# Near scores of a banded attention as products of 32 query columns, with merge loads, merges and strided items at other steps

## The chip, the cores and the metric

The kernel runs on one core of a Trainium2 chip. The metric is the device time in microseconds (us) of one execution, the median of three runs. Engines are named as in the profile: PE is TensorE's matmul, PEld its weight load, DVE is VectorE, ACT is ScalarE, POOL is GpSimd, SP is SyncE, whose queue issues nearly all DMAs here. A row's "L890" is line 890 of the kernel before; the changed kernel's lines are one less from L898 to about L1182.

## The reference, cut to what matters

The reference is one decoder layer for a prompt of 2048 positions and for a small group of samples: norm, one input projection, eight attention heads of width 64 beside a gating unit, an output projection, a SwiGLU feed-forward part. The change lies in the prompt's attention. Each head has three branches with keys at distances 0, d, 2d, ..., w:

```
BRANCHES = ((128, 1), (512, 4), (2048, 16))
...
    s = jnp.einsum('bnqrhc,bnkrhc->bnrhqk', qb, kc).astype(jnp.float32)
    s = s * (HEAD_DIM ** -0.5) + bias_hj[None, None, None]
    s = jnp.where(valid[None, :, None, None], s, NEG_INF)
    lse = jax.nn.logsumexp(s, axis=-1)
    p = jnp.exp(s - lse[..., None])
    o = jnp.einsum('bnrhqk,bnkrhc->bnqrhc', p.astype(vc.dtype), vc)
...
    w = jax.nn.softmax(jnp.stack(lses, axis=0), axis=0)
    return jnp.sum(w[..., None] * jnp.stack(outs, axis=0).astype(jnp.float32), axis=0)
```

The last two lines merge the branches by weights that come from their softmax denominators.

## The kernel before, in words

The program has three parts: the input projection with the samples' attention (to about 561 us of the span), the prompt's attention (561 to 862 us), and the output projection with the feed-forward part (to the end).

**The attention part** works on head pairs p = 0 to 3, two heads of 64 channels side by side in the 128 partitions. A pair has 16 band items n = 0 to 15 of 128 query positions each, which do the branches with d = 1 and d = 4 together, and four strided items "s" of 512 positions, which do the branch with d = 16. Query columns are kept by residue modulo 4: in an item's 128 columns, r * 32 to r * 32 + 31 are the positions of residue r.

A band item passes these steps, all of whose names stand in its rows of the profile:
- `pair_scores`: the scores in one tile `ps_s` for both heads z. "Near" keys are the 256 of this and the preceding block (128 where n is 0), for all 128 query columns of a head in one product (L890). "Far" keys are up to 96 of the same residue in the three blocks before; each residue has its own, so a product takes 32 query columns (L897) and there are four per head. Items n = 0 and 1 have no far keys.
- `band_bias` on DVE (L903) adds the bias and takes the minimum, `band_exp` on ACT, `band_turn` on PE (transposes, L919) with copies on ACT and DVE.
- `band_values` on PE: products with `ve`, the values by block (L942), and with `vf`, the values of far keys (L952); `band_out` copies to `ob`.

A strided item reorders k and q on POOL (`strided_order`, tile `sq`, L967), multiplies (L977), adds the bias and takes minima on DVE, subtracts these on POOL (`strided_sub`, L989, tile `e`), takes exp on ACT (L992), transposes on PE (L1001), multiplies with the values, and copies to `o`.

After a pair's last item the merge weights are worked out from its statistics (`Stats`, tile `f`), stored to the DRAM tile `f_d` (L1073) and read back spread over partitions (`merge_load`, L1087, four calls of two DMAs). A merge is three POOL operations on 256 columns of the pair: L1096 multiplies `ob` by its weight, L1098 multiplies `o`, L1100 adds. After four merges `merge_store` writes half of `ob` to `cat_d` (L1104), which the output projection reads.

**The order** is written out by a plan: `at(step, phase, fn)` puts a call at a step, and within a step phases go in a fixed order. Each engine, and SP's queue of DMA issues, runs its instructions in the order in which the plan issues them. A pair takes NI = 40 steps, two for each item, starting at B0 for p = 0; the items' order is one of the lists `FIRST` (p = 0), `OTHER` (p = 1, 2) and `LAST` (p = 3). The merges of pair p run during the items of pair p + 1, counted in steps from that pair's start, s0. The next pair's tiles are loaded during a pair by five calls of `load`: q, k, the bias b, v by residue, and `ve` in four DMAs. `sgu_sample_cat_load` is a DMA of the samples' gating result (`pair<-cs_d`, L1112), whose transposes on PE stand at step B0 + 22 (L1119). `pair` is a tag with two buffers, used by that load and by the merge loads.

Of the kernel before, what the change touches and what calls it, by code (L numbers as in the profile page):

```python
# [10 lines left out]
F32 = mybir.dt.float32  # L11
# [8 lines left out]
P = 128  # L20
T = 2048
NT = T // P
# [3 lines left out]
C = 64  # L26
# [10 lines left out]
FAR = 96  # L37
BAND = FAR + 2 * P
# [7 lines left out]
class Plan:  # L46
# [8 lines left out]
    def at(self, step, phase, fn, *args):  # L55
        self.events.append((step, self.PHASES.index(phase), self.n, fn, args))
        self.n += 1
# [10 lines left out]
def hymba_step(ctx: ExitStack, tc: tile.TileContext, A: dict, O: dict):  # L68
    nc = tc.nc
    sync, act, dve, pool, pe = nc.sync, nc.scalar, nc.vector, nc.gpsimd, nc.tensor  # L70
# [11 lines left out]
    def ps_s():  # L82
        return psum_s.tile([P, 2, 512], F32, name="ps_s", tag="s", bufs=2)
# [84 lines left out]
    at = plan.at  # L168
# [7 lines left out]
    def pair_tile(dtype=F32R):  # L176
        return rp.tile([P, 2, 512], dtype, name="pair", tag="pair", bufs=2)
# [481 lines left out]
    B0 = 240  # L659
# [4 lines left out]
    for n in range(len(first) + 4):  # L664
        if n >= 4:
            (w_split if first[n - 4][0] == "w" else x_half_split)(*first[n - 4][1:])
        if n < len(first):
            if first[n][0] == "w":
                k = first[n][1]
# [41 lines left out]
    for half in range(2):  # L711
        for ki, kind in enumerate(ORDER[half]):
            for gi, tiles in enumerate(GROUPS):
                start = ((half * 5 + ki) * 3 + gi) * 8
# [72 lines left out]
    i = 0  # L787
# [91 lines left out]

    def pair_scores(*its):  # L880

        d, s = its[0]["d"], ps_s()
        for z, it in enumerate(its):
            n = it["n"]
            m = min(3, max(0, n - 1))
            near = P if n == 0 else 2 * P
            it.update(s=s[:, z, :], c0=FAR - 32 * m if n else FAR + P, m=m)
            half = slice(z * C, z * C + C)
            k0 = (n + 1) * P - near
            pe.matmul(it["s"][:, BAND - near:BAND], d["q"][half, n * P:(n + 1) * P], d["k"][half, k0:k0 + near], start=True, stop=True)  # L890
        for r in range(4):
            for z, it in enumerate(its):
                n, m, half = it["n"], it["m"], slice(z * C, z * C + C)
                if m:
                    k = d["k"][half].rearrange("p (n r i) -> p n r i", r=4, i=32)[:, n - 1 - m:n - 1, r, :]
                    c = n * P + r * 32
                    pe.matmul(it["s"][r * 32:r * 32 + 32, it["c0"]:FAR].rearrange("p (n i) -> p n i", i=32),  # L897
                              d["q"][half, c:c + 32], k, start=True, stop=True)  # L898

    def band_bias(it):  # L900
        d, st, n, z, s, c0 = (it[x] for x in ("d", "st", "n", "z", "s", "c0"))
# [177 lines left out]
    def merge_load(p, j):  # L1079

        if p < HP - 1:
            f = pair_tile(F32)
            t_ = f[:, 0], f[:, 1]
        else:
            t_ = raw_tile(), zn_tile()
        for c in range(2):
            sync.dma_start(t_[c], dap(f_d, (p * 8 + j + c) * 2 * CP * 512, [[512, 2 * CP], [0, C // CP], [1, 512]]))  # L1087
            v = t_[c].rearrange("p (i z r) -> p i z r", z=2, r=NT)
            mf[p, j + c] = v[:, :, 0], v[:, :, 1]
# [45 lines left out]
        (strided_scores if its[0]["kind"] == "s" else pair_scores)(*its)  # L1135

    FIRST = [0, 1, 2, 3, "s", 4, 5, "s", 6, 7, 8, "s", 9, 10, 11, "s", 12, 13, 14, 15]
    OTHER = [0, "s", 1, 2, 3, 4, "s", 5, 6, 7, 8, "s", 9, 10, 11, 12, "s", 13, 14, 15]
    LAST = ["s", 0, 1, "s", 2, 3, "s", 4, 5, "s", 6, 7] + list(range(8, NT))
    units, taken = [], set()  # L1140
    for p in range(HP):
        r4 = 0
# [20 lines left out]
    for p in range(1, HP):  # L1163
        s0 = B0 + (p - 1) * NI
        at(s0 + 4, "misc", begin, p)
        for y in (4, 6, 8, 15, 18):
            at(s0 + y, "misc", load, p)

    def stats_of(p, steps, r0, r1):
# [5 lines left out]
    for p in range(HP):  # L1175
        s0 = B0 + (p + 1) * NI
        if p == HP - 1:
            x = s0 - NI
            stats_of(p, [(x + y, ph) for y, ph in ((26, "early"), (27, "turn"), (28, "early"), (28, "early"), (29, "early"), (29, "mid"))], 0, 64)
            steps = ((2, "early"), (2, "turn"), (3, "early"), (4, "early"), (5, "early"), (5, "early"))  # L1180
            for j in (0, 2):
                at(x + 30, "mid", merge_load, p, j)  # L1182
            for j, y, eng in ((0, 33, dve), (1, 33, pool), (2, 36, dve), (3, 36, pool)):
                for part in range(3):
                    at(x + y + part, "store", merge, p, j, eng, part)
            at(x + 36, "store", merge_store, p, 0, 2)
            at(x + 39, "store", merge_store, p, 2, 4)
        else:
            steps = ((2, "misc"), (3, "misc"), (4, "early"), (5, "early"), (5, "misc"), (6, "mid"))
            fast = p == HP - 2  # L1190
            y0 = 12
            when = [y0 + (i * 2 // 3 if fast else i) for i in range(24)]
            for j in range(0, 8, 2):
                at(s0 + max(8, when[3 * j] - 4) + (j == 2), "mid", merge_load, p, j)
            for i, y in enumerate(when):
                at(s0 + y, "store", merge, p, i // 3, pool, i % 3)
            for j in (0, 4):
                at(s0 + when[3 * j + 11] + 1, "store", merge_store, p, j, j + 4)
        stats_of(p, [(s0 + y, ph) for y, ph in steps], 64 if p == HP - 1 else 0, P)
# [34 lines left out]
    for n in range(3):  # L1234
        at(B0 + 40 + 30 * n, "store", down_plain, n)

    at(B0 + 19, "misc", sgu_sample_cat_load)
    at(B0 + 22, "scores", sgu_sample_cat)

    plan.run(B0)  # L1240
# [1270 lines left out]
```

## The time and the profile before

| what | value |
|---|---|
| runs | 2467.05, 2467.8, 2472.98 us; median 2467.8 us |
| profiled execution | 2461.96 us, its span 2460.2 us |
| granted TensorE clock over the span | 0.974 |
| attention part, by head pair (p = 0, 1, 2, 3) | 68.8, 74.1, 73.5, 84.1 us |
| PE busy over the span | 2350.1 us in 14592 records |
| POOL, DVE, ACT busy over the span | 1438.1, 1482.7, 1203.3 us |

The pairs' stretches are cut where PE reaches a pair's first scores, at 561.5, 630.3, 704.4 and 777.9 us; the last one ends at 862 us, where the output projection is running. In rows of groups, "out<-in" gives the tiles by the program's names, "x" the count, and the bracket the idle time ahead of an instruction with what ended it. "PEclk" is the granted clock as a share of full speed. A time "A:B" is in us from the span's start.

### The profile page before, as it was taken

To read this page: it belongs to the slowest core of one execution; us is meant where nothing else is said; L and a number is where in the kernel's file an instruction comes from. 1 tells how busy PE (TensorE), PEld (TensorE's weight loads), DVE (VectorE), ACT (ScalarE), POOL (GpSimd) and SP (SyncE) were. 2 spreads that over 40 slices of the span, in tenths; PEclk is the share of its full clock that TensorE was granted. 3 is DMA by queue.
4 is the path that set the end of the run, shared out by engine and by line. 5 is a ranking of instruction groups with operands and counts; after the bars stand their busy time and mean duration, and the time that the engine had idled before them with its cause. 6 is when DMAs were issued, how large, how long until landed. Compare 5 with 4: busy or idle time off the path is not lost. (4 is left out here: it accounts for less than half of the span.)

```text
span 2460.2 us, 41718 instructions
## 1 busy us (share of the span) xinstructions
PE 2350.1 (96%) x14592; PEld 2026.5 (82%) x14592; DVE 1482.7 (60%) x2902; ACT 1203.3 (49%) x2745; POOL 1438.1 (58%) x1153
## 2 busy tenths in 40 slices
PE   8999999997988899999999999999999998999998
PEld 6877786665666678999999988999999977999997
DVE  3467573114555534767777676566666666677676
ACT  6424333224555546656665546444443446555555
POOL 2225463112345646888788764756666563888885
PEclk9999999998989898999999999999999998999999
DMA  9864856786554564887877654766666644878552
GB/s 276 248 193 138 247 160 212 226 255 172 143 149 119 153 199 137 256 265 229 256 243 232 209 164 152 262 205 215 200 214 216 212 125 164 271 244 249 172 171 88
DMA packets 333365, 494.61 MB, mean 201 GB/s; under 512 B 42903, under 2 KB 174176, under 8 KB 329572
## 3 DMA queue, kind: packets, MB, share of 16 engines
q1 hardware_dynamic: 326308, 479.90, 63.4%
q10 hardware_dynamic: 6848, 12.06, 1.8%
q8 instruction: 115, 1.88, 0.3%
q14 instruction: 94, 0.77, 0.1%
HBM read 404.72 MB, written 168.98 MB: 233 GB/s over the span
## 5 line engine op out<-in xcount | busy, mean ns | idle before, releaser
L1626 POOL TENSOR_TENSOR op<-fr,op 128x512 fp32r<-128x512 f32 x392 | 522.5, 1342 | 350.6 <-ACT op L1622 262.1
L1863 PE MATMUL ps_m<-xh,op 128*128 128x384 f32 (+3 forms) x1344 | 429.9, 320 | 3.9 <-DVE raw L1874 3.5
L1864 PE MATMUL ps_m<-xl,op 128*128 128x384 f32 (+3 forms) x1344 | 428.6, 319 | 1.6 <-POOL xl L145 1.5
L1865 PE MATMUL ps_m<-xh,op 128*128 128x384 f32 (+3 forms) x1344 | 429.0, 319 | 0.0
L1716 DVE TENSOR_TENSOR acc<-acc,ps_o 128x512 f32<-128x512 f32 x448 | 300.3, 684 | 71.1 <-PE ps_o L1714 63.8
L1714 PE MATMUL ps_o<-hop 128*128 128x512 f32 x1142 | 322.6, 394 | 1.7 <-DVE hop L1695 1.0
L1863 PEld LDWEIGHTS ps_m<-xh,op 128*128 128x128 f32 x1344 | 256.7, 191 | 13.2 <-DVE raw L1874 6.7
L1864 PEld LDWEIGHTS ps_m<-xl,op 128*128 128x128 f32 x1344 | 256.4, 191 | 7.3 <-POOL xl L145 2.0
L1865 PEld LDWEIGHTS ps_m<-xh,op 128*128 128x128 f32 x1344 | 256.3, 191 | 0.0
L1714 PEld LDWEIGHTS ps_o<-hop 128*128 128x128 f32 x1142 | 209.4, 188 | 37.7 <-DVE hop L1695 2.8
L1622 ACT ACTIVATE op<-fr 128x512 fp32r<-128x512 f32 x396 | 239.3, 621 | 0.0
L325 PE MATMUL ps_s<-wh,xh 128*128 128x512 f32 x480 | 197.1, 411 | 6.1 <-ACT xh L142 6.0
L326 PE MATMUL ps_s<-wl,xh 128*128 128x512 f32 x480 | 190.0, 396 | 0.0
L327 PE MATMUL ps_s<-wh,xl 128*128 128x512 f32 x480 | 189.7, 395 | 0.0
L1863 PE MATMUL ps_t<-xh,op 128*128 128x384 f32 (+2 forms) x560 | 180.7, 323 | 5.5 <-ACT xh L1512 2.5
L1864 PE MATMUL ps_t<-xl,op 128*128 128x384 f32 (+2 forms) x560 | 179.9, 321 | 0.5 <-DVE xl L1534 0.3
L1865 PE MATMUL ps_t<-xh,op 128*128 128x384 f32 (+2 forms) x560 | 179.9, 321 | 0.0
L546 POOL TENSOR_TENSOR pr<-kv,qb 96x512 f32<-96x512 f32 x32 | 46.5, 1452 | 158.1 <-DMA kv<-in_cache_k_dram 77.0
L1695 POOL TENSOR_TENSOR hop<-hop 128x512 fp32r<-128x512 f32 x96 | 130.9, 1364 | 11.9 <-ACT hop L1691 11.4
L325 PEld LDWEIGHTS ps_s<-wh,xh 128*128 128x128 f32 x480 | 91.6, 191 | 41.4 <-issue 16.8
L1714 PE MATMUL ps_m<-hop 128*128 128x512 f32 x384 | 119.5, 392 | 0.0
L1877 ACT ACTIVATE zn<-zn 128x384 f32<-128x384 f32 (+2 forms) x65 | 31.6, 487 | 171.5 <-DVE zn L1876 171.5
(568 smaller groups left out, 5391.3 us busy)
## 6 DMA issues: line engine op xcount, KB each, us to landing
fr<-ab_d SPq DMA_DIRECT2D x308, 256.0 KB
hop<-dd_d SPq DMA_DIRECT2D x143, 256.0 KB
out_ks_dram<-in_cache_k_dram SPq DMA_DIRECT2D x56, 512.0 KB
out_vs_dram<-in_cache_v_dram SPq DMA_DIRECT2D x56, 512.0 KB
ab_d<-fr SPq DMA_DIRECT2D x88, 256.0 KB
dwx<-dd_d SPq DMA_DIRECT2D x71, 256.0 KB
ab_d<-pair SPq DMA_DIRECT2D x63, 256.0 KB
kv<-in_cache_k_dram SPq DMA_DIRECT2D x64, 192.0 KB
```

The costliest lines, as they stand in the source:

```text
L325: pe.matmul(o[j], xh[:, k, :], wh, start=(k == 0), stop=False)
L326: pe.matmul(o[j], xh[:, k, :], wl, start=False, stop=False)
L327: pe.matmul(o[j], xl[:, k, :], wh, start=False, stop=(k == KD - 1))
L546: eng.tensor_mul(pr[0:n], x[0:n], q[0:n])
L1622: act.activation(ops[f, j][0], ab[f][j], AF.Copy)
L1626: (pool if f > 1 or j in POOL_LOW[f] or B.b0 else dve).tensor_sub(lo_, ab[f][j], hi.bitcast(F32))
L1695: (pool if B.b0 or k >= 7 * (NF // 2 - 1) else dve).tensor_sub(lo_, lo_.bitcast(F32), hi.bitcast(F32))
L1714: pe.matmul(ps, l_, r_, start=(new and y == 0), stop=(y == 2), skip_group_check=True)
L1716: dve.tensor_add(x[:, cs], x[:, cs], ps)
L1863: pe.matmul(out, wh[:, ks], xh[:, :, k], start=(k == 0 and q not in (2, 4, 6)), stop=False, skip_group_check=True)
L1864: pe.matmul(out, wh[:, ks], xl[:, :, k], start=False, stop=False, skip_group_check=True)
L1865: pe.matmul(out, wl[:, ks], xh[:, :, k], start=False, stop=(k == 3), skip_group_check=True)
```

## The change

It has two parts. The near scores of an item are issued as four products of 32 query columns per head, each with all 256 (or 128) near keys, in the way of the far ones; first the eight near products, then the eight far ones. And calls stand at other steps:
- strided items come later in a pair's list (`OTHER`: after items 2, 6, 9 and 12 in place of 0, 4, 7 and 11; `LAST`: not at its head);
- `sgu_sample_cat_load` stands at B0 + 2 in place of B0 + 19;
- the four `merge_load` calls of a pair stand at s0 + 7 to s0 + 10 in place of four steps ahead of their merges, the later two in a new tile `mf` with two buffers; the merges start at s0 + 15 (14 for p = 2) in place of s0 + 12;
- the next pair's first three loads (q, k, b) stand at s0 + 11, 12, 13 in place of 4, 6, 8, where p > 1;
- in the last pair's merges, two that were DVE's are POOL's, at other steps, and the store of two is split in two.

The diff:

```
     def pair_scores(*its):
-        d, s = its[0]["d"], ps_s()
+        d, s, n = its[0]["d"], ps_s(), its[0]["n"]
+        m = min(3, max(0, n - 1))
+        near = P if n == 0 else 2 * P
+        c0 = FAR - 32 * m if n else FAR + P
         for z, it in enumerate(its):
...
-            pe.matmul(it["s"][:, BAND - near:BAND], d["q"][half, n * P:(n + 1) * P], d["k"][half, k0:k0 + near], start=True, stop=True)
-        for r in range(4):
-            for z, it in enumerate(its):
...
+            it.update(s=s[:, z, :], c0=c0, m=m)
+        for far in range(1 + (m > 0)):
+            for r in range(4):
+                for z, it in enumerate(its):
+                    half, c, rows = slice(z * C, z * C + C), n * P + r * 32, slice(r * 32, r * 32 + 32)
+                    if far:
+                        out = it["s"][rows, c0:FAR].rearrange("p (n i) -> p n i", i=32)
+                        k = d["k"][half].rearrange("p (n r i) -> p n r i", r=4, i=32)[:, n - 1 - m:n - 1, r, :]
+                    else:
+                        out, k = it["s"][rows, BAND - near:BAND], d["k"][half, (n + 1) * P - near:(n + 1) * P]
+                    pe.matmul(out, d["q"][half, c:c + 32], k, start=True, stop=True)
...
-            f = pair_tile(F32)
+            f = pair_tile(F32) if j < 4 else ap_.tile([P, 2, 512], F32, name="mf", tag="mf", bufs=2)
...
-    OTHER = [0, "s", 1, 2, 3, 4, "s", 5, 6, 7, 8, "s", 9, 10, 11, 12, "s", 13, 14, 15]
-    LAST = ["s", 0, 1, "s", 2, 3, "s", 4, 5, "s", 6, 7] + list(range(8, NT))
+    OTHER = [0, 1, 2, "s", 3, 4, 5, 6, "s", 7, 8, 9, "s", 10, 11, 12, "s", 13, 14, 15]
+    LAST = [0, 1, "s", 2, "s", 3, 4, "s", 5, "s", 6, 7] + list(range(8, NT))
...
-        for y in (4, 6, 8, 15, 18):
+        for y in (11, 12, 13, 15, 18) if p > 1 else (4, 6, 8, 15, 18):
             at(s0 + y, "misc", load, p)
...
-            for j, y, eng in ((0, 33, dve), (1, 33, pool), (2, 36, dve), (3, 36, pool)):
+            for j, y, eng in ((0, 33, dve), (1, 33, pool), (2, 35, pool), (3, 38, pool)):
...
-            at(x + 39, "store", merge_store, p, 2, 4)
+            at(x + 39, "store", merge_store, p, 2, 3)
+            at(x + 42, "store", merge_store, p, 3, 4)
...
-            y0 = 12
+            y0 = 14 if fast else 15
             when = [y0 + (i * 2 // 3 if fast else i) for i in range(24)]
             for j in range(0, 8, 2):
-                at(s0 + max(8, when[3 * j] - 4) + (j == 2), "mid", merge_load, p, j)
+                at(s0 + 7 + j // 2, "mid", merge_load, p, j)
...
-    at(B0 + 19, "misc", sgu_sample_cat_load)
+    at(B0 + 2, "misc", sgu_sample_cat_load)
```

**SP's queue in the first pair.** The DMA issues around the load of `cs_d`, in SP's order, before (`v_d` is the DRAM copy of the values, `zn` its source tile):

```order
L366 DMA v_d<-zn 128x4x128 x2
L849 DMA ve<-v_d 32x6x128 x4
L878 DMA vf<-v_d 96x4x512
L845 DMA v<-v_d 128x2048
L857 DMA q<-qk_d 128x2048
L878 DMA vf<-v_d 96x4x512
L857 DMA k<-qk_d 128x2048
L860 DMA b<-b_d 128x2x480
L845 DMA v<-v_d 128x2048
L849 DMA v<-v_d 32x16x128 x4
L1112 DMA pair<-cs_d 32x1024
```

and with the change:

```order
L366 DMA v_d<-zn 128x4x128 x2
L1111 DMA pair<-cs_d 32x1024
L849 DMA ve<-v_d 32x6x128 x4
L878 DMA vf<-v_d 96x4x512
L845 DMA v<-v_d 128x2048
```

The load of `cs_d` moved from behind the four loads of the second pair's values to directly behind the store of `v_d`; the others kept their order.

**SP's queue in the second pair.** From the weights' store (`f_d<-f`) to the last load of merge weights, before:

```order
L857 DMA q<-qk_d 128x2048
L1073 DMA f_d<-f 8x16x32 x8
L857 DMA k<-qk_d 128x2048
L1087 DMA pair<-f_d 128x1x512 x2
L860 DMA b<-b_d 128x2x480
L878 DMA vf<-v_d 96x4x512
L1087 DMA pair<-f_d 128x1x512 x2
L845 DMA v<-v_d 128x2048
L849 DMA ve<-v_d 32x16x128 x4
L1087 DMA pair<-f_d 128x1x512 x2
L1104 DMA cat_d<-ob 128x1024
L1087 DMA pair<-f_d 128x1x512 x2
```

and with the change:

```order
L1072 DMA f_d<-f 8x16x32 x8
L1086 DMA pair<-f_d 128x1x512 x4
L878 DMA vf<-v_d 96x4x512
L1086 DMA mf<-f_d 128x1x512 x4
L857 DMA q<-qk_d 128x2048
L857 DMA k<-qk_d 128x2048
L860 DMA b<-b_d 128x2x480
L845 DMA v<-v_d 128x2048
L849 DMA ve<-v_d 32x16x128 x4
L1103 DMA cat_d<-ob 128x1024
```

All eight loads of merge weights now stand behind the weights' store and ahead of the third pair's loads.

**POOL at the second pair's first merges**, before (`sm` is of the statistics, `sq` the reordered k and q, `e` a strided item's subtraction, `ob` and `o` the merge):

```order
L1034 TENSOR_TENSOR sm<-st,sel_g 128x512
L989 TENSOR_TENSOR e_5889<-e_5889,st 128x512
L989 TENSOR_TENSOR e_5897<-e_5897,st 128x512
L967 COPY sq<-k 128x512
L967 COPY sq<-q 128x512
L1096 TENSOR_TENSOR ob<-ob,pair 128x256
L1098 TENSOR_TENSOR o_5295<-o_5295,pair 128x16x16
L1100 TENSOR_TENSOR ob<-ob,o_5295 128x256
L989 TENSOR_TENSOR e_6094<-e_6094,st 128x512
L1096 TENSOR_TENSOR ob<-ob,pair 128x256
L989 TENSOR_TENSOR e_6099<-e_6099,st 128x512
```

and with the change:

```order
L966 COPY sq<-k 128x512
L966 COPY sq<-q 128x512
L988 TENSOR_TENSOR e_6087<-e_6087,st 128x512
L988 TENSOR_TENSOR e_6096<-e_6096,st 128x512
L966 COPY sq<-k 128x512
L966 COPY sq<-q 128x512
L1095 TENSOR_TENSOR ob<-ob,pair 128x256
L1097 TENSOR_TENSOR o_5333<-o_5333,pair 128x16x16
L1099 TENSOR_TENSOR ob<-ob,o_5333 128x256
L1095 TENSOR_TENSOR ob<-ob,pair 128x256
L988 TENSOR_TENSOR e_6323<-e_6323,st 128x512
L1097 TENSOR_TENSOR o_5333<-o_5333,pair 128x16x16
L988 TENSOR_TENSOR e_6333<-e_6333,st 128x512
```

The copies of the second strided item and the first item's subtractions changed places, and `sm` (the statistics of the pair before) now stands ahead of both. The first merge still stands behind the first strided item and ahead of the second one's subtractions.

**PE at the second pair's start**, before (L919 and L942 to L952 are transposes and values of the first pair's last items, L977 is a strided item's scores, L1040 belongs to the statistics):

```order
L890 MATMUL ps_s<-k,q 128x128 x2
L919 MATMUL ps_t_5817<-ident,e 128x128 x3
L919 MATMUL ps_o_5822<-ident,e 128x128 x3
L942 MATMUL ps_o_5826<-pt,ve 64x256 x2
L942 MATMUL ps_o_5826<-pt,ve 64x128 x4
L952 MATMUL ps_o_5826<-pt,vf 64x32 x16
L977 MATMUL ps_s<-sq 128x128 x8
L919 MATMUL ps_t_5868<-ident,e 128x128 x3
L919 MATMUL ps_t_5873<-ident,e 128x128 x3
L1040 MATMUL ps_o_5877<-sel_r,sm 128x16 x4
L890 MATMUL ps_s<-k,q 128x256 x2
```

and with the change:

```order
L897 MATMUL ps_s<-k,q 32x128 x8
L918 MATMUL ps_t_5916<-ident,e 128x128 x3
L918 MATMUL ps_o_5921<-ident,e 128x128 x3
L941 MATMUL ps_o_5925<-pt,ve 64x256 x2
L941 MATMUL ps_o_5925<-pt,ve 64x128 x4
L951 MATMUL ps_o_5925<-pt,vf 64x32 x16
L897 MATMUL ps_s<-k,q 32x256 x8
L918 MATMUL ps_t_5967<-ident,e 128x128 x3
L918 MATMUL ps_t_5972<-ident,e 128x128 x3
L1039 MATMUL ps_o_5979<-sel_r,sm 128x16 x4
L897 MATMUL ps_s<-k,q 32x256 x8
L897 MATMUL ps_s<-k,q 32x32 x8
```

In place of the strided item's scores, item 1's stand second, and two wide products of an item are eight narrow ones.

More of the change, by code (lines that the diff above doesn't have):

```diff
@@ L880, in pair_scores @@
     def pair_scores(*its):
-        d, s = its[0]["d"], ps_s()
+        d, s, n = its[0]["d"], ps_s(), its[0]["n"]
+        m = min(3, max(0, n - 1))
+        near = P if n == 0 else 2 * P
+        c0 = FAR - 32 * m if n else FAR + P
         for z, it in enumerate(its):
[L884 to L890, printed above, removed]
-        for r in range(4):
-            for z, it in enumerate(its):
[L893 to L898, printed above, removed]
+            it.update(s=s[:, z, :], c0=c0, m=m)
[9 more added lines that the diff above has]
+                    pe.matmul(out, d["q"][half, c:c + 32], k, start=True, stop=True)
     def band_bias(it):
```

## The prediction

> **What bounds the kernel now.** I read the page first, then the busy time by stretch in the attention part, then each hole in PE's work there and what ended it. The page has PE as the engine that is nearly always at work:
>
> ```profile
> PE 2350.1 (96%) x14592; PEld 2026.5 (82%) x14592; DVE 1482.7 (60%) x2902; ACT 1203.3 (49%) x2745; POOL 1438.1 (58%) x1153
> ```
>
> The change touches only the attention part. Its windows, one for each head pair, and a quiet stretch of 20 us inside the first:
>
> ```profile
> core 0: us, PE busy (x) PEld busy (x) DVE busy (x) ACT busy (x) POOL busy (x), PEclk, DMA share, GB/s
> 561.50:630.30 68.80, 54.17 (x765) 40.20 (x764) 34.89 (x98) 36.62 (x103) 16.75 (x16) 0.88 0.61 165
> 630.30:704.40 74.10, 61.85 (x865) 45.75 (x864) 40.96 (x118) 38.65 (x110) 36.73 (x41) 0.88 0.62 156
> 704.40:777.90 73.50, 62.18 (x863) 45.99 (x862) 39.60 (x113) 38.53 (x109) 36.69 (x41) 0.88 0.59 152
> 777.90:862.00 84.10, 73.99 (x973) 54.19 (x974) 47.90 (x143) 46.72 (x128) 50.41 (x54) 0.90 0.43 125
> 620.00:640.00 20.00, 19.57 (x303) 15.19 (x304) 12.12 (x38) 12.27 (x36) 6.35 (x6) 1.00 0.42 133
> ```
>
> In the last row PE is busy 98% at a clock of 1.00, and no other engine passes 61%. So PE bounds the attention part where nothing stalls it. By pair it is not so: PE is idle 14.6, 12.3, 11.3 and 10.1 us, and the granted clock is 0.88 to 0.90. The holes, each window cut from the start of a hole in PE's work to the return of the clock:
>
> ```profile
> 589.14:606.30 17.16, 6.00 (x46) 5.41 (x46) 1.87 (x6) 2.73 (x9) 0.00 (x0) 0.60 0.59 112
> 641.40:647.30 5.90, 4.07 (x41) 3.24 (x42) 4.73 (x17) 3.87 (x12) 1.84 (x2) 0.71 0.11 17
> 657.14:664.30 7.16, 4.77 (x37) 3.05 (x36) 2.78 (x8) 4.40 (x12) 5.09 (x6) 0.76 1.06 231
> 675.78:688.20 12.42, 5.89 (x43) 4.30 (x44) 3.02 (x8) 4.88 (x13) 8.32 (x10) 0.59 0.76 220
> 715.67:722.40 6.73, 4.90 (x46) 3.66 (x48) 4.93 (x18) 3.93 (x13) 1.83 (x2) 0.75 0.12 18
> 731.69:739.40 7.71, 6.21 (x47) 4.62 (x48) 3.33 (x10) 4.88 (x13) 4.17 (x5) 0.56 1.08 217
> 750.12:759.90 9.78, 3.63 (x29) 2.38 (x30) 2.25 (x6) 3.12 (x8) 6.06 (x8) 0.65 0.82 282
> ```
>
> A hole costs its idle time (length less PE busy) and half of what PE then does at half clock; the time at half clock is 2 x (1 - PEclk) x length, or PE's busy time where that is less. First row: 11.16 idle, and 6.00 busy all at half clock, so 3.0; together 14.2. The others, in order: 3.5, 4.1, 9.4, 3.5, 4.6 and 8.0. All seven come to 47.3 us, 31.4 of it idle and 15.9 clock. The 641 row shows that 1.83 us of idle time is enough to lower the clock.
>
> [...]
>
> **The load of `cs_d`: -14.2 us.** SP's issues, then PE's first use:
>
> ```profile
> 574.66 15.58 SPq L849 DMA_DIRECT2D v<-v_d  x4
> 590.28 4.72 SPq L1112 DMA_DIRECT2D pair<-cs_d  x1
> ```
>
> ```profile
> 600.30 1.03 PE L1119 MATMUL ps_t<-ident,pair 32*128 32x32 f32 x8 [11.16 <-DMA pair<-cs_d]
> ```
>
> The load stands behind 15.58 us of issuing `ve`, whose first use is a whole pair later. `cs_d` itself is written by an issue (L617) that stands ahead of the whole part on SP. The change issues the load ahead of the first pair's `ve`, near 564 us, so it lands near 574 (590.28 to 600.30 is 10 us), 15 us and more before PE reaches its transposes at 589. Its issue takes 4.72 us, which fits in SP's idle time there, from the end of `v_d<-zn` to the next issue:
>
> ```profile
> 562.40 0.94 SPq L366 DMA_DIRECT2D v_d<-zn  x2
> 568.16 2.37 SPq L849 DMA_DIRECT2D ve<-v_d  x4
> ```
>
> That is 4.82 us wide, so the `ve` behind it is late by nothing to 1 us. I take nothing; the whole hole goes.
>
> **Strided items away from the pair's start: -7.0 us.** At 641 and 715 PE waits for a score buffer that DVE has not read yet:
>
> ```profile
> PE ps_s L890 <- DVE st L903: 1.8, 1, 1.8
> ```
>
> DVE is busy 4.73 of 5.90 us there, with the strided item's bias and minima beside the statistics of the pair before. With item 1 in second place and the strided item fourth, DVE has an item's bias less at that point. Both holes go (3.5 each); if DVE is late all the same, nothing is won, so 0 to -7.
>
> **Merge loads ahead of the merges: -26.1 us.** The holes at 657, 675, 731 and 750 have one chain, shown at 680 us:
>
> ```profile
> 655.32 0.73 POOL L1096 TENSOR_TENSOR ob<-ob,pair 128x256 f32<-128x256 f32 x1 [12.08 <-DMA pair<-f_d]
> ```
>
> ```profile
> 679.88 0.72 POOL L1096 TENSOR_TENSOR ob<-ob,pair 128x256 f32<-128x256 f32 x1 [6.60 <-DMA pair<-f_d]
> 680.56 1.04 POOL L989 TENSOR_TENSOR e<-e,st 128x512 f32<-128x512 f32 x1
> 681.55 0.87 POOL L1098 TENSOR_TENSOR o<-o,pair 128x256 f32<-128x256 f32 x1
> 681.63 0.63 ACT L992 ACTIVATE e<-e 128x512 f32<-128x512 f32 x1 [6.38 <-POOL e L989]
> ```
>
> ```profile
> 682.31 1.11 PE L1001 MATMUL ps_t<-ident,e 128*128 128x128 f32 x4 [6.53 <-ACT e L992]
> ```
>
> A merge waits on POOL for its weights; the strided item's subtraction stands behind it, then ACT's exp and PE's transposes. The weights are late because `pair` has two buffers and the later loads stand on SP behind the next pair's `ve`:
>
> ```profile
> 642.36 5.04 SPq L1073 DMA_DIRECT2D f_d<-f  x8
> ...
> 653.28 15.31 SPq L849 DMA_DIRECT2D ve<-v_d  x4
> ```
>
> With four buffers (two of `pair`, two of `mf`) all eight loads stand directly behind the weights' store. The second, third and fourth merges' weights then come with the first's, and 4.1 + 9.4 + 4.6 + 8.0 = 26.1 us go.
>
> **A new wait at the first merge: +5 us.** The weights' store starts 12.1 us into the pair (642.36 less 630.30), and the first merge could start 13.0 us after it (655.32), so about 24 to 25 us into the pair whatever the order. The merges now begin at step 15; a pair without holes takes some 57 us, 1.43 a step, so POOL reaches the first merge at 21.4 us and waits 3 us. Behind it are the other merges and six subtractions. POOL has 36.7 us of work in a pair (window row), of which up to 34 stand behind that wait, and 33 us are left. Its lag can reach PE by a strided item: nothing, if there is slack (the 12.08 us wait at 655 cost PE 4.1), or 3 us with the clock. I take 2.5 for each of two pairs.
>
> **Near scores: -11 us.** One item's near and far products, and item 0's near alone:
>
> ```profile
> 624.53 0.66 PE L1001 MATMUL ps_t<-ident,e 128*128 128x128 f32 x4
> 625.12 0.70 PE L890 MATMUL ps_s<-k,q 64*128 64x256 f32 x4
> 625.75 0.40 PE L897 MATMUL ps_s<-k,q 64*32 64x96 f32 x16
> 626.07 0.66 PE L1001 MATMUL ps_o<-ident,e 128*128 128x128 f32 x4
> ```
>
> ```profile
> 630.27 0.49 PE L890 MATMUL ps_s<-k,q 64*128 64x128 f32 x4
> 630.70 0.33 PE L919 MATMUL ps_t<-ident,e 128*128 128x128 f32 x1
> ```
>
> From start to start, 256 near keys take 0.63 us and 128 take 0.43: 0.20 for 128 keys and 0.23 fixed. The far products take 0.32 for 96 keys, 0.15 by that rate, and 0.17 fixed. Narrow near products of four residues and two heads take the same keys, and their 16 records are no more than the far's. If near and far run as one sequence with one fixed part, they take 0.40 + 0.15 + 0.17 = 0.72 in place of 0.95, a gain of 0.23; if each pays its own, 0.89, a gain of 0.06. The two groups now have one shape, and the far's 16 show no pause inside, so I take 0.19, nearer the first. With far keys there are 14 x 4 = 56 items: 10.6. The other 8 gain 0.06 each: 0.5. Ends: 4 and 13 us.
>
> **The last pair's end: +4 us.** The output projection's first weights wait for SP:
>
> ```profile
> 846.59 0.63 ACT L142 ACTIVATE op<-v 128x512 fp32r<-128x512 f32 x1 [5.79 <-DMA v<-in_w_out_dram]
> ```
>
> ```profile
> SPq L1104 <- POOL ob L1100: 51.0, 5, 18.5
> ```
>
> Stores to `cat_d` hold up SP until POOL's merge is done. With the change the store of the third pair's second half stands directly ahead of loads of the output weights on SP, and the last pair's merges are all but one POOL's. I count 3 us later and some clock; bounds 0 and 8. The next pair's loads, now behind the merge loads, cost nothing while `ve` (15.31 us of issue) ends before the next pair: issued from step 18, about 26 us in, it ends at 41 of 57.
>
> **Sum:** -14.2 - 7.0 - 26.1 + 5 - 11.1 + 4 = -49.4 us. The profiled execution took 1.8 us around its 2460.2 us span, 2461.96, 0.24% under the runs' median; by it 2412.6, and by the median of 2467.8 it is 2418.4.
>
> **Rivals.**
>
> POOL becomes the limit. By the count above it has 34 us of work for 33 us; if it lags, all the six strided items behind the merge in two pairs wait, about 2 us and 1.7 of clock each: 22 us come back, 2440. For it: POOL was the waiting link in four holes. Against: it was busy only 50% of a pair.
>
> The next pair's loads come late, being issued 7 steps later behind eight more loads. A hole like that at 675, 8 us and 3.4 of clock, in two pairs: 23 us back, 2441. Against: 16 us of slack by the count above.
>
> Slower: PE is bound by its number of records, not by their width. The quiet stretch runs 303 records in 20.00 us, 66 ns each; the change adds 12 records to each of 64 items, 768 in all. If each took 66 ns more, it is +50.7: -47.3 + 50.7 + 9 = +12.4, 2480. It decides if a narrow record costs more than about 50 ns.
>
> [...]
>
> Against this rival stand 16 far records in 0.32 us, 20 ns each, and a run of 60:
>
> ```profile
> 622.28 0.40 PE L897 MATMUL ps_s<-k,q 64*32 64x96 f32 x16
> 622.60 1.09 PE L942 MATMUL ps_o<-pt,ve 128*64 128x256 f32 x12
> 623.52 1.08 PE L952 MATMUL ps_o<-pt,vf 96*64 96x32 f32 x32
> ```
>
> These take 2.25 us, 37 ns each, with no wait.
>
> **Chances.** The forecast 0.66, POOL as the limit 0.15, late loads 0.10, the record bound 0.05, and 0.04 that holes of like size turn up elsewhere and nothing is won. The forecast's own range goes by the ends of its terms: near 4 in place of 11 (+7), holes at the pairs' starts kept (+7), not both; downwards no new waits (-9) and near 13 (-2): 2407 to 2432. Holding 8 in 10, the range takes in both rivals at 2440 and 2441 with their own spread, to 2446, and a few us below for holes that I left alone: 2404 to 2446. About 7 us, 0.3%, can be told from no change here: faster 0.91 (the first three cases), same 0.04, slower 0.05.
>
> **What would show it.** PE at L1119 without a wait and the clock at 1.00 around it; no hole of 1.8 us at the pairs' starts; POOL's merges waiting for `f_d` under 5 us once in each pair; the second and third pairs at about 57 us; an item's near and far scores 0.72 to 0.77 us from start to start; 15360 PE records; ACT at L142 waiting about 8 us. I am wrong if near records of 32 columns come at 40 ns and more, if subtractions on POOL stand late behind merges without a DMA to wait for, or if `ve` or q and k end a wait of PE.

## The result, and the profile after

The changed kernel takes 2436.61 us (median of 4 runs, 2427.75 to 2445.07) against 2469.82 us for the one before in the same comparison: a ratio of 0.9865, 95% interval 0.9823 to 0.9907. It is 33 us faster. The forecast was 2418, a gain of 49 us, so the sign and the range hold and about 16 us of the gain are missing.

In the profiled executions shown here the attention part begins anywhere from 559 to 570 us, in kernels whose first part is the same. Much of the 10 us and more by which runs of one kernel spread comes from there: the profiled execution that begins this part first, at 559.0 us, is 10.7 us under its kernel's median, and the one that begins it last, at 570.1, is 8.8 over. So traces are compared below by the length of a pair's stretch and not by where it ends. "Tail" is the last pair up to the first product of the output projection (before: 777.9 to 855.9 us, 78.0).

The windows of the four pairs after the change:

```profile
core 0: us, PE busy (x) PEld busy (x) DVE busy (x) ACT busy (x) POOL busy (x), PEclk, DMA share, GB/s
562.90:620.00 57.10, 49.93 (x955) 38.35 (x954) 34.77 (x98) 36.33 (x101) 14.62 (x14) 0.94 0.76 197
620.00:683.10 63.10, 55.93 (x1056) 42.99 (x1054) 39.30 (x118) 38.94 (x111) 36.87 (x41) 0.97 0.71 181
683.10:744.90 61.80, 55.06 (x1058) 42.07 (x1056) 38.04 (x113) 38.47 (x109) 38.98 (x43) 1.00 0.71 177
744.90:823.00 78.10, 62.60 (x1113) 47.66 (x1113) 43.52 (x126) 45.30 (x124) 52.91 (x57) 0.89 0.44 137
```

The first three pairs fell from 68.8, 74.1 and 73.5 us to 57.1, 63.1 and 61.8; the tail did not fall. The clock is back at 0.94 to 1.00 in the first three. But the second and third were forecast at about 57, and PE is still idle 7.2 and 6.7 us in them.

The large holes did go as forecast. PE's transposes of `cs_d` wait for nothing of it, and POOL's wait for the first pairs' merge weights, 46.4 us before, is 3.8:

```profile
593.40 0.68 PE L1118 MATMUL ps_t<-ident,pair 32*128 32x32 f32 x8 [0.31 <-ACT eT L1002]
```

```profile
POOL ob L1095 <- DMA pair<-f_d: 3.8, 3, 1.6
```

What PE waits for now, in order of time: the first pair's `v`, then twice "issue", which means that nothing in the profile held it, then two waits in the tail:

```profile
583.02 1.33 PE L1009 MATMUL ps_o<-eT,v 128*64 128x128 f32 x10 [4.54 <-DMA v<-v_d]
...
665.34 0.83 PE L951 MATMUL ps_o<-pt,vf 96*64 96x32 f32 x21 [2.27 <-issue]
...
726.37 0.79 PE L897 MATMUL ps_s<-k,q 64*32 64x256 f32 x21 [1.55 <-issue]
...
802.20 1.43 PE L897 MATMUL ps_s<-k,q 64*32 64x256 f32 x32 [4.83 <-DVE st L902]
...
814.11 1.85 PE L918 MATMUL ps_t<-ident,e 128*128 128x128 f32 x6 [5.78 <-ACT e L907]
```

The first of these was 2.02 us before; the two for issue are new. Here are two items' scores and what follows them:

```profile
649.00 0.83 PE L897 MATMUL ps_s<-k,q 64*32 64x256 f32 x32
650.08 0.66 PE L1000 MATMUL ps_t<-ident,e 128*128 128x128 f32 x4 [0.24 <-ACT e L991]
650.66 0.83 PE L897 MATMUL ps_s<-k,q 64*32 64x256 f32 x32
651.42 0.66 PE L1000 MATMUL ps_o<-ident,e 128*128 128x128 f32 x4
```

From 650.66 to 651.42 an item's near and far scores take 0.76 us in place of 0.95: the 0.19 of the forecast, to the hundredth. The item at 649.00 is busy as short (0.83 us in both rows), but behind it PE waited 0.24 us for ACT, and its gain is gone. So the products are shorter, and the second and third pair are still some 5 us longer than forecast.

### The profile page after: what moved, and what is told of

Its sections match the earlier page's. It is cut to its first block, busy times and chain, and to the rows that moved or that the text cites. A ratio compares the mean times of both kernels' runs of the same rounds, so it can differ in the third digit from the quotient of the medians.

```text
span 2430.4 us, 43270 instructions
## 1 busy us (share of the span) xinstructions
PE 2330.8 (96%) x15360; PEld 2020.0 (83%) x15360; DVE 1472.4 (61%) x2899; ACT 1202.2 (49%) x2745; POOL 1440.4 (59%) x1156
```

## The experiments

Theory at this point: the three moves of the order are worth what was forecast, and the near products' 11 us are lost to something that comes with them. The rival: the near products are worth their 11 us and the moves fell short.

**Near scores alone, taken out and put in.** The first run has the changed kernel with the wide near product again ("the wide form" from here on; "narrow" is the form of the change):

```
-                        out, k = it["s"][rows, BAND - near:BAND], d["k"][half, (n + 1) * P - near:(n + 1) * P]
-                    pe.matmul(out, d["q"][half, c:c + 32], k, start=True, stop=True)
...
+            pe.matmul(it["s"][:, BAND - near:BAND], d["q"][half, n * P:(n + 1) * P], d["k"][half, k0:k0 + near], start=True, stop=True)
```

> The changed kernel with the near scores as one product of 128 query columns per head again; all else as changed. If the near term of the forecast is right (0.20 us less from start to start for each of 56 items), it is about 11 us slower than the changed kernel, and the waits of PE for issue near 663 and 725 us stay. If those waits come of the added records, they go and it is only 4 to 6 us slower.

Measured: 2431.86 us (2424.33 to 2433.71), ratio to before 0.9852 (0.9828 to 0.9875). It is not slower than the changed kernel but 5 us faster by the medians, the intervals overlapping. Its windows:

```profile
562.70:617.80 55.10, 51.47 (x763) 37.70 (x762) 34.81 (x98) 36.47 (x102) 14.57 (x14) 0.97 0.75 205
617.80:677.90 60.10, 57.09 (x863) 42.17 (x862) 39.47 (x118) 38.64 (x111) 36.90 (x41) 1.00 0.71 179
677.90:738.20 60.30, 57.05 (x865) 42.07 (x864) 38.14 (x113) 38.53 (x109) 38.94 (x43) 1.00 0.73 182
738.20:816.90 78.70, 66.40 (x922) 48.86 (x921) 43.88 (x127) 45.62 (x125) 52.27 (x56) 0.87 0.50 144
```

PE is busy more in the third pair (57.05 against 55.06, the narrow products' gain of 2.0) and idle less (3.3 against 6.7): the pair is shorter by 1.5 us. Over all four the wide form is 5.9 us shorter. It has no wait for issue of 0.3 us or more, and the wait for `v` is back at its old size:

```profile
580.40 1.70 PE L1010 MATMUL ps_o<-eT,v 128*64 128x128 f32 x16 [2.07 <-DMA v<-v_d]
```

The second run has the kernel before with the new near products and nothing else:

```
-            pe.matmul(it["s"][:, BAND - near:BAND], d["q"][half, n * P:(n + 1) * P], d["k"][half, k0:k0 + near], start=True, stop=True)
...
+                        out, k = it["s"][rows, BAND - near:BAND], d["k"][half, (n + 1) * P - near:(n + 1) * P]
+                    pe.matmul(out, d["q"][half, c:c + 32], k, start=True, stop=True)
```

> The kernel before with the near scores alone changed. By the forecast's term 11 us faster than before. The rival: PE reaches each old wait earlier and waits longer there (four holes end by a DMA whose time does not depend on PE), so the gain ahead of such a hole is lost and 4 to 6 us are left.

Measured: 2468.53 us, ratio 1.0003 (0.9993 to 1.0013): nothing, less than even the rival allowed. The old holes took the gain, and some grew past it:

```profile
586.52 1.76 PE L1009 MATMUL ps_o<-eT,v 128*64 128x128 f32 x14 [4.01 <-DMA v<-v_d]
...
607.75 1.03 PE L1118 MATMUL ps_t<-ident,pair 32*128 32x32 f32 x8 [10.64 <-DMA pair<-cs_d]
...
688.59 1.12 PE L1000 MATMUL ps_t<-ident,e 128*128 128x128 f32 x4 [7.37 <-ACT e L991]
```

These were 2.02, 11.16 and 6.53 us. So in two surroundings the near products are worth nothing or less, and the three moves make all of the gain.

**The load of `cs_d` alone**, in the kernel before:

```
-    at(B0 + 19, "misc", sgu_sample_cat_load)
+    at(B0 + 2, "misc", sgu_sample_cat_load)
```

> The kernel before with the load of cs_d alone moved to B0 + 2. By the forecast 14.2 us faster, the hole at 589 gone and nothing behind it late. The rival, from the profile after: the load's issue and bytes delay the first pair's v, PE's wait for v at 577 grows from 2.0 to 4.5 us with 3.4 us more at half clock, and only 9 to 10 us are won.

Measured: 2452.33 us (2441.66 to 2462.83) against 2467.62, ratio 0.9931 (0.9911 to 0.9951): 15 us faster, 12 to 22 by the interval. The rival falls, since PE's wait for `v` stays at 2.03 us and its transposes of `cs_d` wait for nothing:

```profile
576.65 1.09 PE L1010 MATMUL ps_o<-eT,v 128*64 128x128 f32 x16 [2.03 <-DMA v<-v_d]
...
585.29 0.68 PE L1119 MATMUL ps_t<-ident,pair 32*128 32x32 f32 x8
```

The grown wait for `v` after the change therefore came with the near products, not with this load.

**The strided items' places alone**: the wide form with the old list for the second and third pair.

```
-    OTHER = [0, 1, 2, "s", 3, 4, 5, 6, "s", 7, 8, 9, "s", 10, 11, 12, "s", 13, 14, 15]
+    OTHER = [0, "s", 1, 2, 3, 4, "s", 5, 6, 7, 8, "s", 9, 10, 11, 12, "s", 13, 14, 15]
```

> The changed kernel with wide near scores (the run near_wide) and, in the second and third pair, the strided items at their places of before. By the forecast's term a hole of 1.8 us with 3.4 us at half clock comes back at each of the two pairs' starts: 7 us slower than near_wide. The rival: the later places have waits of their own (in near_wide PE waits for strided transposes and values 0.7 us at a time, three times a pair), so that it is only 2 to 3 us slower.

Measured: 2433.54 us, ratio 0.9878 (0.9844 to 0.9911); against the wide form it is 1.7 us slower by the medians and 6 by the ratios, which does not tell 7 from 2. The trace does better: from the second pair's start to the output projection 203.3 us against 199.0, so 4.3 us. Both holes are back, but only the second one with a lower clock:

```profile
633.02:639.00 5.98, 3.73 (x48) 2.68 (x48) 4.93 (x18) 4.06 (x13) 1.82 (x2) 1.00 0.11 16
695.41:701.60 6.19, 4.35 (x43) 3.59 (x44) 4.94 (x18) 3.81 (x12) 1.85 (x2) 0.72 0.12 18
```

**The merge loads alone**, in the kernel before, with the merges' start and the later loads of q, k and b:

```
+            f = pair_tile(F32) if j < 4 else ap_.tile([P, 2, 512], F32, name="mf", tag="mf", bufs=2)
...
+        for y in (11, 12, 13, 15, 18) if p > 1 else (4, 6, 8, 15, 18):
...
+            y0 = 14 if fast else 15
...
+                at(s0 + 7 + j // 2, "mid", merge_load, p, j)
```

> The kernel before with, alone, the merge loads moved together with their new tile, the merges' later start and the later loads of q, k and b. By the forecast's terms -26.1 for the four holes and at most +5 for a new wait of POOL and +4 at the end: 17 to 22 us faster than before. If POOL is the limit, its waits for f_d are gone and the subtractions still come late: under 10 us faster.

Measured: 2450.71 us against 2464.41 in the same comparison, ratio 0.9951 (0.9933 to 0.9969): 14 us by the medians, 8 to 16.5 by the interval. The expected 17 to 22 lies just outside it. POOL's wait for `pair` fell from 46.4 us to this:

```profile
POOL ob L1096 <- DMA pair<-f_d: 2.2, 1, 2.2
```

The rival on POOL expected under 10 us; the medians and the second pair, 65.9 us in place of 74.1, speak against it, though the interval's lower end does not shut it out. Part of the rest went into a wait for issue of 1.81 us, here with wide near products, and part into the tail, where the two waits are 4.71 and 6.14 us and were 3.10 and 0.95:

```profile
699.65 0.47 PE L897 MATMUL ps_s<-k,q 64*32 64x96 f32 x2 [1.81 <-issue]
...
830.26 1.23 PE L890 MATMUL ps_s<-k,q 64*128 64x256 f32 x4 [4.71 <-DVE st L903]
...
843.66 1.85 PE L919 MATMUL ps_t<-ident,e 128*128 128x128 f32 x6 [6.14 <-ACT e L908]
```

**What comes with the near products: instructions.** The profile's page lists a DMA queue q8 of the kind "instruction", whose packets are 16 KB each (1.88 MB in 115). Before:

```profile
q8 instruction: 115, 1.88, 0.3%
```

With the narrow near products, here after the change:

```profile
q8 instruction: 121, 1.98, 0.3%
```

The six more packets are there in each kernel with narrow products and in none with wide ones; over the second and third pair 9 and 8 pass after the change, 8 and 6 in the wide form. Six packets for 768 more products and as many weight loads are 256 instructions in each. At 256, the 14592 products and 14592 weight loads of the kernel before make 114 packets, where the page has 115: by this estimate the queue brings PE's instructions. In the window from 662.1 to 663.8 us of the changed kernel one such packet passed, taking 5.8% of 16 engines for 1.7 us, 1.6 us on its engine; PE stopped at 663.07 and went on at 665.34, 1.6 us after the packet's end:

```profile
q8 instruction: 1, 0.02, 5.8%
```

All traces of this study together hold 15 waits for issue of 0.78 us or more on PE in the attention part. Each ends 1.3 to 1.7 us after the end of such a packet, and so do seven smaller ones of 0.3 us and more. Some 30 packets pass in that part of a trace (27 before the change and 35 after it, from 561 to 862 us), most of them without a wait. So I read these waits as PE out of instructions until the next 16 KB are in. What makes a packet late I took to be the small pieces of `ve`, and spread those:

```
-            load_values(d["vb"], p, False)
-            yield
+            for r in range(4):
+                load_values(d["vb"], p, False, r0=r)
+                yield
...
-        for y in (11, 12, 13, 15, 18) if p > 1 else (4, 6, 8, 15, 18):
+        for y in (11, 12, 13, 15, 18, 23, 28, 33) if p > 1 else (4, 6, 8, 15, 18, 23, 28, 33):
```

> The changed kernel (narrow near scores) with the four loads of ve issued five steps apart, not back to back. Theory: PE's waits for issue (2.3 us near 663, 1.5 near 725) are its own instructions, 16 KB at a time on a queue of their own, coming late behind the 512-byte pieces of ve; with pieces spread they shrink under 0.5 us and the second and third pair get 2 to 3 us shorter each, 4 to 6 us in all. The rival, that 768 more records hold PE up wherever they stand: the waits stay, in size if not in place.

Measured: 2433.28 us, ratio 0.9881 (0.9851 to 0.9911), no difference from the changed kernel. Waits for issue of 1.8 and 1.5 us in sum remain (4.2 after the change), one of them in the first pair where there was none:

```profile
PE ps_s L898 <- issue: 1.8, 2, 1.7
PE ps_o L952 <- issue: 1.5, 1, 1.5
```

The theory of `ve` falls; the rival of this run, that the added records hold PE up wherever they stand, is the nearer one. What makes a packet late stays open.

The third pair of this run shows more. Its clock is 1.00 and its waits for issue are 0.2 us, so nothing of the theory of instructions is left in it, and yet it gains nothing:

```profile
684.08:744.46 60.38, 55.01 (x1056) 42.07 (x1055) 37.94 (x113) 38.51 (x109) 39.04 (x43) 1.00 0.70 181
```

PE is busy 2.0 us less than in the wide form's third pair (57.05 of 60.30 us), and idle 2.1 us more, almost all of it in waits for ACT and DVE (5.1 us in place of 2.9), most of them at strided items. Shorter products bring PE sooner to results of ACT and DVE that are not there yet.

**The first pair's `v` first.** In the changed kernel such a packet also passed between the issue of the first pair's `v` and PE's use of it; in the wide form none did in that time. The window is 572.3 to 583.0 us of the changed kernel:

```profile
q8 instruction: 1, 0.02, 1.1%
```

So `v` was issued ahead of the second part of `ve`, in both forms:

```
-            for n0, n1 in ((0, 10), (10, NT)):
-                load_values(d["vb"], 0, False, n0, n1)
-                yield
+            load_values(d["vb"], 0, False, 0, 10)
+            yield
         d["vp"] = value_tile(2 * p)
         load_values(d["vp"], p, True)
         yield
+        if p == 0:
+            load_values(d["vb"], 0, False, 10, NT)
+            yield
```

> The changed kernel with the first pair's v by residue issued ahead of the second part of its ve. Theory: narrow near products lose in the first pair because the 16 KB of instructions they need early pass between that v and its landing; with v issued 2.5 to 3 us sooner PE's wait there falls from 4.5 us to under 2, and the first pair from 57.1 to 50 to 53 us. If something else holds that pair, it stays at 55 to 57.

> The same with wide near products. The wait of 2.1 us and its 3.4 us at half clock go: the first pair from 55.1 to 51 to 52 us. By the theory the narrow form is now at least level with this one in the first pair (its products are 2.6 us shorter there) and still behind in the second, where its waits for issue are: over the attention part narrow less wide between -3 and +3 us, not -11.

Measured: narrow 2434.02 us, ratio 0.9856 (0.9833 to 0.9880); wide 2422.54 us, ratio 0.9807 (0.9785 to 0.9828). The intervals do not overlap. PE's wait for `v` is gone in both. The first pair is 54.1 us narrow and 52.6 wide, each a little above its expectation. Over the attention part narrow is 10.7 us longer, well outside the 3 us that I expected, and it is 1.5 us longer in the first pair, where I expected it level. First the second and third pair of the wide form, then those of the narrow one:

```profile
619.30:679.60 60.30, 57.16 (x863) 42.06 (x862) 39.49 (x118) 38.65 (x111) 36.85 (x41) 1.00 0.72 165
679.60:739.90 60.30, 57.05 (x865) 42.05 (x864) 38.13 (x113) 38.54 (x109) 39.03 (x43) 1.00 0.75 195
```

```profile
619.00:684.00 65.00, 57.22 (x1055) 44.12 (x1054) 39.31 (x118) 39.01 (x111) 36.79 (x41) 0.95 0.71 179
684.00:747.70 63.70, 56.85 (x1060) 43.50 (x1060) 38.05 (x113) 38.62 (x109) 38.99 (x43) 0.97 0.70 161
```

Here the narrow form's waits for issue are 5.4 us in sum over the attention part. The clock is lowered in both of its rows (0.95 and 0.97), in the second pair at the longest of these waits (2.76 us, ended at 664.79), so that PE is busy as long as in the wide form (57.22 and 57.16 us in the second pair) although its products are shorter.

**The tail.** Three attempts. First, the early loads of `cat_d` two steps later, in the changed kernel:

```
-    for i, y in ((1, -9), (2, -9), (3, -8), (4, -5)):
+    for i, y in ((1, -7), (2, -7), (3, -6), (4, -5)):
```

> The changed kernel with the early loads of cat_d for the output projection (cr) two steps later, so that on SP they stand behind the loads of output weights and no longer ahead of two of them. If the store to cat_d holds up these weights through SP, the 5.8 us wait of PE at 808 us goes with its clock: 6 to 8 us faster than the changed kernel. If the weights are late for another reason, or the loads of cat_d are what is late next, no change.

Measured: 2436.41 us, ratio 0.9881 (0.9855 to 0.9908): no change. The wait for the output weights is gone and one of 5.29 us for the next load takes its place, as the rival said:

```profile
827.66 0.79 PE L1416 MATMUL ps_m<-op,pair 128*128 128x512 f32 x1 [5.29 <-ACT pair L1407]
```

Second, in the wide form, the third pair's merges closer together, DVE's merge later and the last pair's first store later:

```
-            when = [y0 + (i * 2 // 3 if fast else i) for i in range(24)]
+            when = [y0 + (i * 3 // 5 if fast else i) for i in range(24)]
...
-            for j, y, eng in ((0, 33, dve), (1, 33, pool), (2, 35, pool), (3, 38, pool)):
+            for j, y, eng in ((0, 35, dve), (1, 33, pool), (2, 35, pool), (3, 38, pool)):
...
-            at(x + 36, "store", merge_store, p, 0, 2)
+            at(x + 38, "store", merge_store, p, 0, 2)
```

> near_wide with the third pair's merges run a little faster so that their second store stands ahead of the weights' store of the last pair on SP, DVE's merge two steps later, and the last pair's first store two steps later. If the 4.6 us wait at 804 is that store's landing, held on SP in front of the output weights, and the 4.2 us wait at 792 is DVE's merge in front of the bias, both go with their clock: 8 to 14 us faster than near_wide. If what is next late (the load of cat_d for the output projection) takes their place, 0 to 4 us.

Measured: 2425.87 us, ratio 0.9849 (0.9819 to 0.9880), 6 us under the wide form by the medians and 1 by the ratios, so not clear of the spread. DVE's wait is gone, the one for the output weights is 7.17 us, and the tail is 75.4 us in place of 78.7.

```profile
806.23 1.85 PE L919 MATMUL ps_t<-ident,e 128*128 128x128 f32 x6 [7.17 <-ACT e L908]
```

Third, both of these and `v` first, with either form of the near products:

> Wide near products, v first, the third pair's merges ended sooner, DVE's merge later, and the early loads of cat_d behind the output weights on SP. The two ends tried apart each left the other's load late (7.2 us at 799, 5.3 us at 822); together both should go: 6 to 10 us less than the run tail_fix, about 2417. If the loads only trade places again: 2422 and more.

> The same with narrow near products. With most waits on DMAs gone PE's own work should show: if the forecast's 0.20 us for an item were worth its sum it would be 11 us under all_wide; by the theory that instruction loading takes it back, within 4 us of it, with waits of PE for issue of 3 us and more in sum that all_wide doesn't have.

Measured: wide 2422.84 us, ratio 0.9813 (0.9789 to 0.9837); narrow 2430.39 us, ratio 0.9838 (0.9812 to 0.9864). The two are told apart by the trace rather than by the runs. The tails are 74.2 and 74.6 us, 4 to 5 shorter than in the runs with `v` first alone; here is the wide one's:

```profile
738.60:812.80 74.20, 63.92 (x921) 47.06 (x920) 41.97 (x125) 44.49 (x122) 52.76 (x57) 0.92 0.54 155
```

But the wide one is no faster than with `v` first alone, and lands on the second number of its expectation. From the tail's end to the feed-forward part's first product it takes 139.0 us, where that run takes 136.2: what the tail gains is largely waited for in the output projection. For the narrow form the attention part is 5.3 us longer than for the wide one, and its waits for issue sum to 5.0 us, where the wide one has none; the forecast had it 11 us shorter.

## Why the prediction was right and wrong

**What held, and by what luck.** The sign, the range and the worth of the moves held: the wide form, which leaves the near term out, is 35.8 us faster than before where the sum without that term says 38.3. The near term failed. The changed kernel still lies in the stated range because that had been widened to 2446 for two rivals which did not occur; by the ends of the forecast's own terms, 2407 to 2432, its 2436.6 lies outside.

**What bounds the kernel.** The seven holes and their cost held, with the half clock behind them as counted (in the kernel before PEclk is 0.50 from 600.30 to 606.30 us, behind the hole of `cs_d`, and 0.50 from 682.30 to 686.00): they are gone or small. That PE alone bounds a pair without them did not. It was read from 20 us in which PE is busy 98%; over the wide form's second and third pair, at full clock, it is busy 95% (57.09 of 60.10 us and 57.05 of 60.30), and the rest is mostly waits for ACT and DVE, which take up what PE saves.

**The load of `cs_d`** (-14.2): 15.3 us alone. Right, and nothing behind it was late: PE's wait for `v` stayed at 2.03 us.

**Strided items** (-7.0): 4.3 us by the trace. Both holes do belong to the old places, but one of the two did not lower the clock when it came back, and the new places have small waits of their own. The term was too large by 2 to 3 us.

**Merge loads** (-26.1, with +5 and +4 against it): alone 14 us (8 to 16.5) where the three terms say -17: just past the interval's end, and by a different path. The new wait at the first merge, +5, did not come: POOL waited 3.8 us in three waits, at most 1.6. The weights' store starts 8.5 us into the third pair (691.70 less 683.15) and not 12.1, because the strided item at the pair's start, which I had moved one paragraph earlier, had also delayed it; with the old list it starts at 12.1 in the second pair. And the first merge follows the store's start by 10.2 us, not by the 13.0 that I had taken from the kernel before, where loads of other tiles stood between. With the old list POOL's merges of these pairs wait for nothing although the store is as late as before, so the early store is not the whole reason.

```profile
691.70 5.01 SPq L1072 DMA_DIRECT2D f_d<-f  x8
```

**The last pair's end** (+4) was too small for the waits at the end, and yet the tail as a whole hardly grew. Those waits are 12.3 us (4.83 + 5.78 + 1.72) and were 5.1, and at them 20.5 us run at half clock where 13.7 did. From the start of the first of them to the output projection the wide form takes 25.0 us where the kernel before takes 19.3, so +5.6; the narrow form takes 25.6, and 3.7 us at half clock follow. The mechanism was near: on SP a load of `cat_d` (L1393) waits for the store to `cat_d` to land, and the loads of output weights stand behind it. ACT at L142 then waits 9.5 us, where about 8 was forecast.

```profile
SPq L1393 <- DMA cat_d<-ob: 10.8, 2, 7.1
```

The part I left out was DVE's merge, which waits for its weights in front of an item's bias: 7.03 us after the change, 6.4 in the wide form and 5.3 before. Something else went the other way: ahead of these waits the tail takes 53.7 us in the wide form where it took 58.6, with its small holes near 800 us gone. So the tail as a whole is 78.7 us, and was 78.0.

**The near scores** (-11.1) are the step that failed. Each number of it was right: 0.76 us from start to start where 0.72 to 0.77 was forecast, and PE busy 2.0 us less in the third pair. What failed is the step from an item to a sum, that PE's time saved is the kernel's time saved. Put in alone they gave nothing (1.0003); in three pairs of kernels that differ only in them, the narrow form is 5, 11 and 8 us slower by the medians (3, 12 and 6 by the ratios), in the second pair clear of the spread. In the kernel before, the old holes, most of which a DMA ends directly or through POOL and ACT, take the gain: PE gets there sooner and in two of them waits longer (4.01 us for 2.02, 7.37 for 6.53). For the three pairs the traces show where the gain goes, over the attention part, narrow less wide, in us, from one trace of each kernel (PE's work is its busy time less half of what it does at half clock):

| | changed kernel | `v` first | `v` first and tail |
|---|---|---|---|
| PE's work at full clock | -9.1 | -9.8 | -9.3 |
| waits for ACT and DVE | +8.0 | +8.4 | +6.8 |
| waits for issue | +4.2 | +5.4 | +5.0 |
| half clock | +0.7 | +7.4 | +3.4 |
| wait for the first pair's `v` | +2.5 | 0 | 0 |
| smaller gaps | -0.3 | -0.7 | -0.6 |
| attention part | +5.9 | +10.7 | +5.3 |

So the work did shrink by nearly what was forecast. Waits for ACT and DVE take back most of that; in the third pair of the run with spread `ve` they take all of it, with hardly a wait for issue and the clock at 1.00. Waits for issue (4.2 to 5.4 us in the table; in five of six kernels with narrow products) and the lowered clock (0.7 to 7.4) make the rest, and turn no gain into a loss.

The longer wait for `v` fits the packet beside it: in the four narrow kernels with the old order of `v` one passes between its issue and PE's use, 8.5 to 10.6 us later, and in the six wide ones none does and the use comes after 8.0 to 8.4 us; this was not isolated.

**The rivals.** POOL as the limit and late loads of the next pair did not occur. The bound by PE's number of records did not come as it was put, since PE's work at full clock fell. But 768 more records, and as many weight loads, have to be brought in, by my reading of the 121 packets in place of 115, and that the forecast had at nothing: 4 to 5.4 us of waits for issue and part of the clock. In all, the step from -11 to +5 to +11 is 16 to 22 us, 21 to 29 ns a record. I had turned this rival down with the 20 ns at which far records follow each other, which shows how fast PE executes sixteen of them and nothing on how fast hundreds arrive or on what PE waits for behind them. The 32 score records of an item, near and far, take 0.76 us, 24 ns each, where the rival needed narrow records of about 50 ns.

**The sum.** By stretches of the profiled executions, the wide form against the kernel before, in us:

| stretch | forecast without the near term | measured |
|---|---|---|
| first pair (`cs_d`) | -14.2 | -13.7 |
| second and third pair (-7.0 - 26.1 + 5) | -28.1 | -27.2 |
| tail | +4 | +0.7 |
| attention part | -38.3 | -40.2 |

The profiled executions differ by 37.7 us over the whole span, the runs by 35.8. That the sum comes so near is in part luck: the strided term was too large and the new wait did not come, and the tail's end cost more and its start less. The rest of the miss is the near term, -11 forecast and about nothing to +11 measured.

A version that beats both kernels by the medians is the wide form with `v` first: 2422.54 us, 47 us under before (ratio 0.9807, 0.9785 to 0.9828) and 14 under the changed kernel, whose interval it overlaps by a hair.

## What to carry to other kernels

Time saved on the engine that is busy 98% of a stretch is the kernel's time only if what it waits for next comes no later (here 9.1 to 9.8 us less work of PE gave an attention part 5.3 to 10.7 us longer), so list the next wait of that engine before a gain is multiplied by its count. A stretch without large holes can still have many small waits, and shorter work on one engine can go into them whole, as in the third pair of the run with spread `ve`: 2.0 us less busy, 2.1 us more idle. More and smaller instructions for the same work came here with six more 16 KB packets of the instruction queue and, in five of six kernels, with waits for issue of 0.8 to 2.8 us: look at these packets on the page, and at waits for issue right behind them, before instructions are split. And when a term removes a stall, redo the later terms with the times that hold without it.

## What the runs showed of the hardware

PE stopped in mid-stream without anything in the profile to wait for: 15 waits of 0.8 to 2.8 us, each ending 1.3 to 1.7 us after a 16 KB packet of the instruction queue. I read them as PE out of instructions. Of the 15, 13 are in kernels with narrow products, where instructions are many and small, and two in the run with the merge loads alone, with wide products.

A hole of 1.83 us lowered the clock in one place and not in another: PEclk 1.00 and 0.72 in the two windows of the strided items' run, at holes of 1.83 and 1.85 us, and 0.71 at the hole of 1.83 us at 641 us in the kernel before. What makes the difference, no run shows. So a hole's clock cost of 1.7 us is not certain, and a sum over several should count it in part.
